# Layer 0 of a two-layer decoder trunk: low parts through ScalarE and adding transfers, wide products from group 4 on, matmuls in runs of three

## The chip, the cores and the metric

The kernel runs on one core of one Trainium2 chip. The metric is the device time of one execution in microseconds (us); less is better. The engines are TensorE (PE, with its weight loads listed apart as PEld), VectorE (DVE), ScalarE (ACT), GpSimd (POOL) and SyncE (SP). Here POOL and SP mostly issue transfers.

## The reference

A causal two-layer trunk runs over 512 positions of width 1024 in float32. Each layer is a residual mixer and then a gated feed-forward block; the change touches the feed-forward block of layer 0 alone.

```python
D_MODEL, SEQ, D_FF, DEPTH = 1024, 512, 2816, 2

def gated_conv_ffn(x, w_gate, w_up, conv_w, conv_b, w_down):
    g = jnp.einsum('bsd,df->bsf', x, w_gate)
    g = causal_dwconv3(g, conv_w) + conv_b
    up = jnp.einsum('bsd,df->bsf', x, w_up)
    return jnp.einsum('bsf,fd->bsd', jax.nn.silu(g) * up, w_down)

for layer in range(DEPTH):
    h = h + mixer(rms_norm(h, norm_mix[layer]))
    h = h + gated_conv_ffn(rms_norm(h, norm_ffn[layer]), ...)
return rms_norm(h, final_norm)
```

## The kernel before

**Precision.** Every float32 operand is split into a high part `hi` (rounded to the matmul's input type) and a low part `lo = x - hi`. A product is `hi*hi + hi*lo + lo*hi`. The split is made in two ways. `halves` and `split`: ACT copies `hi`, DVE subtracts `lo`. `summed`: ACT writes `lo = -x` rounded, a transfer on POOL's queue adds x to it in memory (`accum_op=ALU.add`), and ACT copies `hi`; DVE has no part in it.

**Feed-forward block (class `Ffn`).** The 2816 hidden rows are 22 tiles of 128. They are computed in steps f = 0, 2, 4, ..., 20 of two tiles each (`STEPS`). Step 0 is computed directly. In the others gate (`g`) and up (`u`) each take seven block products instead of eight (a Winograd form of Strassen's scheme on 2 x 2 blocks): `prepare(f)` builds weight sums (`s12`, `s34`), `block_sums(kp)` builds the sums of the token blocks (`t41`, `t23`) once, and `products(f)` multiplies. The seven products of a key share three PSUM banks a, b and e (`BANK`); the running sum in bank a or e must be copied out (evacuated) before the next product of that bank begins. ACT copies the first half of a bank to `rows` or `kept` (line 944), DVE adds what is to be added (line 932).

**Narrow and wide.** In a narrow product (line 705) each of four k-tiles takes three matmuls of 256 columns. In a wide one (line 695) the moving operand holds `hi` and `lo` side by side: one matmul of 512 columns with the weight's high part and one of 256 columns with its low part, so 8 instructions for 12. The second half of the bank must then be added too, one more DVE instruction of 128x256. `FIRST_WIDE[layer]` gives the step from which each key is wide (at the gate's first wide step, `u` is wide in products 2, 5 and 3 only).

**Order of the matmuls.** `todo` lists the 14 products of a step. In layer 0 the low matmuls of one product and the next stand together, then the high ones of two (runs of two); in layer 1, where all 14 are wide, runs of three low and three high parts alternate.

**After the products.** Convolution and SiLU give the activation rows `s`; `split_acts` calls `act`, which makes `a_hi` (ACT, line 265) and `a_lo` (DVE, line 267), four buffers of each. `half_down` projects rows already split through half of the output columns (`project`, lines 156 to 158; tile `d` in layer 0, `dn` in layer 1), after each step's products.

**What sets the order.** A scheduler fixes one order of instructions for each engine before the run; each engine takes its list strictly in that order. So an instruction that waits holds up all that stands behind it on its engine. Transfers of raw weights go through SP's queue as one of four `raw` buffers comes free; adding transfers go through POOL's.

Of the kernel before, what the change touches and what calls it, by code (L numbers as in the profile page):

```python
# [9 lines left out]
F32R = mybir.dt.float32r  # L10
BF16 = mybir.dt.bfloat16
AF = mybir.ActivationFunctionType
ALU = mybir.AluOpType
PSUM = bass.MemoryType.PSUM

P = 128
D = 1024
S = 512
# [3 lines left out]
NF = FF // P  # L22
# [9 lines left out]
def tile_trunk(ctx: ExitStack, tc: tile.TileContext, x, norm_mix, norm_ffn, final_norm,  # L32
# [3 lines left out]
    nc = tc.nc  # L36
# [44 lines left out]
    def behind(ins, first):  # L81

        if first is not None:
            tc.add_manual_dep(ins.ins, first.ins.name, mybir.DependencyInfo(
                mybir.DependencyClass.NoSync, mybir.DependencyReason.DATA), reason="order")
# [176 lines left out]
    def split(pool, src, name, scale=1.0, tag="a", bufs=None):  # L262
        hi = pool.tile([P, S], F32R, tag=f"{tag}hi", bufs=bufs, name=f"{name}_hi")
        lo = pool.tile([P, S], F32R, tag=f"{tag}lo", bufs=bufs, name=f"{name}_lo")
        nc.scalar.activation(hi, src, AF.Copy, scale=scale)  # L265
        if isinstance(scale, float):
            nc.vector.tensor_tensor(lo, src, hi.bitcast(F32), ALU.subtract)
        else:
            nc.vector.scalar_tensor_tensor(lo, src, scale, hi.bitcast(F32),
                                           op0=ALU.mult, op1=ALU.subtract)  # L270
        return hi, lo
# [15 lines left out]
    def padded_tile():  # L287
        turn[0] += 1
        return padded[turn[0] % NPADDED]
# [382 lines left out]
    PAIRS = [k for i in range(NP) for k in (i, i + NP)]  # L672

    FIRST_BY_DMA = 4
    FIRST_WIDE = ({"g": 6, "u": 8}, {"g": 4, "u": 6})

    BANK = {1: "a", 6: "a", 7: "a", 4: "a", 5: "e", 3: "e", 2: "b"}

# [37 lines left out]
    class Ffn:  # L716
# [33 lines left out]
            return s  # L750

        def act(self, ft, s):
            self.acts[ft] = split(self.ap, s, f"a{self.layer}_{ft}", tag="a", bufs=4)

        def pair_weights(self, order):

# [42 lines left out]
        def block_sums(self, kp):  # L799

            n, g1, h1 = f"{self.layer}_{kp}", self.prm("ffn", kp + NP), h[kp + NP]
            t = self.ap.tile([P, 4, HALF], F32, tag="sum", bufs=3, name=f"t{n}")
            b11, b12 = t[:, 2, :], t[:, 3, :]
            first = nc.scalar.activation(t[:, 2:, :], h[kp].rearrange("p (a b) -> p a b", a=2),
                                         AF.Copy, scale=self.prm("ffn", kp))
            if kp > 0:
                behind(first, self.first_sums)
            nc.vector.scalar_tensor_tensor(t[:, 1, :], h1[:, HALF:], g1, b12, op0=ALU.mult,
                                           op1=ALU.subtract)
            nc.vector.tensor_tensor(t[:, 0, :], t[:, 1, :], b11, ALU.add)  # L810
            nc.vector.tensor_tensor(b12, b12, b11, ALU.subtract)
            nc.vector.scalar_tensor_tensor(b11, h1[:, :HALF], g1, t[:, 0, :], op0=ALU.mult,
                                           op1=ALU.subtract)
            self.t23[kp] = self.sums(kp)
            t41 = self.ap.tile([P, 2, 2, HALF], F32R, name=f"t41_{n}")
            self.t41[kp], self.t41both[kp] = (t41[:, 0], t41[:, 1]), t41
            for (hi, lo), src in ((self.t41[kp], t[:, 2:, :]), *(
                    ((both[:, 0], both[:, 1]), t[:, i, :]) for i, both in enumerate(self.t23[kp]))):
                if kp > 1:
                    self.halves(hi, lo, src)  # L820
                    continue
                behind(nc.scalar.activation(lo, src, AF.Copy, scale=-1.0), self.first_sums)
                nc.gpsimd.dma_start(lo, src, accum_op=ALU.add)
                behind(nc.scalar.activation(hi, src, AF.Copy), self.first_sums)
# [87 lines left out]
        def products(self, f, stat):  # L912

            layer, ap, n = self.layer, self.ap, f"{self.layer}_{f}"
            banks = {"g": {}, "u": {}}
            kept = ap.tile([P, 3, HALF], F32, tag="kept", bufs=1, name=f"kept{n}")
            pads = [padded_tile() for _ in range(2)]
            lo, hi = slice(2, 2 + HALF), slice(2 + HALF, 2 + S)
            dst = {("g", 1): pads[0][:, lo], ("g", 6): pads[0][:, hi], ("g", 7): pads[1][:, hi],
                   ("g", 4): pads[1][:, lo]}  # L920
            dst.update({("u", product): kept[:, i, :] for i, product in enumerate((1, 6, 7))})
            onto = {2: 1, 7: 7, 3: 6}
            s = {}

            def in_both(key, product):
                first = FIRST_WIDE[layer]
                return f >= first[key] or f == first["g"] and product in (2, 5, 3)

            def add(d, bank, halves):
                ins = None  # L930
                for half in halves:
                    ins = nc.vector.tensor_tensor(d, bank[:, half * HALF : (half + 1) * HALF], d,
                                                  ALU.add)
                return ins

            def after(key, product, bank):
                halves = range(1 + in_both(key, product))
                if product in onto:
                    ins = add(dst[key, onto[product]], bank, halves)
                    if product == 7:  # L940
                        self.added[key] = ins
                elif (key, product) != ("u", 4):
                    d = dst[key, 7 if product == 5 else product]
                    nc.scalar.copy(d, bank[:, :HALF])
                    add(d, bank, halves[1:])

            todo = [("g", 1), ("u", 1), ("g", 2), ("g", 5), ("g", 6), ("u", 5), ("u", 6),
                    ("g", 7), ("u", 2), ("u", 7), ("g", 3), ("u", 3), ("g", 4), ("u", 4)]
            if layer and all(in_both(*at) for at in todo):
                parts_of = [(0, (False,))]  # L950
                for i in range(0, len(todo), 3):
                    parts_of += [(j, (True,)) for j in range(i, min(i + 3, len(todo)))]
                    parts_of += [(j, (False,)) for j in range(i + 1, min(i + 4, len(todo)))]
            else:
                parts_of = [(i, (i % 2 == 1, i % 2 == 0)) for i in range(len(todo))]
            begun = set()
            for i, lows in parts_of:
                key, product = todo[i]
                bank = self.multiply(banks[key], f"{key}{n}", product, stat[key, product],
                                     in_both(key, product), lows)  # L960
                if len(lows) == 1 and i not in begun:
                    begun.add(i)
                    continue
                after(key, product, bank)
                if (key, product) in (("g", 4), ("g", 3)):
                    j = product == 4
                    row = pads[j][:, 2:]
                    nc.vector.tensor_tensor(row, row, self.r, ALU.mult)  # L968
                    s[j] = self.silu(self.conv(pads[j], f + j), f + j)
                    if j and layer == 0:  # L970
                        nc.vector.tensor_tensor(s[1], s[1], self.r, ALU.mult)
            if layer == 0:
                nc.vector.tensor_tensor(kept[:, :2, :], kept[:, :2, :],
                                        self.r.rearrange("p (a b) -> p a b", a=2), ALU.mult)
            s0 = s[0].rearrange("p (a b) -> p a b", a=2)
            nc.vector.tensor_tensor(s0, kept[:, :2, :], s0, ALU.mult)
            nc.vector.tensor_tensor(s[1][:, HALF:], kept[:, 2, :], s[1][:, HALF:], ALU.mult)
            last = bank[:, :HALF]
            if in_both("u", 4):
                last = kept[:, 0, :]  # L980
                nc.scalar.copy(last, bank[:, :HALF])
                add(last, bank, (1,))
            nc.vector.tensor_tensor(s[1][:, :HALF], last, s[1][:, :HALF], ALU.mult)
            return [(f + 1, s[1]), (f, s[0])]
# [53 lines left out]
    def mixer1(norm):  # L1038
        w = w_in_odd[0]
        with tc.tile_pool(name="m1", bufs=1) as mp:  # L1040
# [156 lines left out]
            for kp in range(NP):  # L1197
                block_sums(kp)
# [144 lines left out]
    def ffn1(norm):  # L1343
        with tc.tile_pool(name="f1", bufs=1) as ap:
# [108 lines left out]
            def product(p, i, c0=0, c1=512, bank=None):  # L1453
# [14 lines left out]
                return ps  # L1468

            vec, act, pool = nc.vector, nc.scalar, nc.gpsimd  # L1470
            rows_f = [wp.tile([P, D], F32, tag="raw", bufs=4, name=f"yf{t}") for t in range(NT)]
            factor, root = ([ssf[:, t, i : i + 1] for t in range(NT)] for i in (4, 5))
# [181 lines left out]
```

## Time and profile before

| | |
|---|---|
| median of 3 runs | 966.77 us (966.71 to 966.88) |
| the profiled execution's own time | 966.66 us |
| its span, first to last instruction | 964.9 us |
| PE busy | 956.6 us (99%) |
| PEld busy | 826.5 us (86%) |
| DVE busy | 847.2 us (88%) |
| ACT busy | 620.8 us (64%) |
| POOL busy | 162.4 us (17%) |
| granted TensorE clock | 0.999 |

The products of layer 0 run from 165.99 us (step 2) to about 450 us (end of those of step 20), those of layer 1 from 644.78 us. Where one engine is busy for 99% of the span, a change moves the time only by what it takes from that engine's work or by the waits that it puts into it. A timeline row gives start, length, engine, line, operation, tiles and shape; lengths of matmuls that follow one another overlap, so distances between starts are what counts. Rows of POOL's own transfers show only the issue; the landing is in the list of transfers.

### The profile page before, as it was taken

What the parts mean: (1) busy time and instruction counts of PE and PEld (TensorE: products, weight loads), DVE (VectorE), ACT (ScalarE), POOL (GpSimd) and SP (SyncE); (2) the same over time, 40 slices, a digit from 0 to 9 for tenths busy, and PEclk for the clock granted to TensorE, in tenths of its full rate; (3) what the DMA queues carried; (4) which work ended last, traced back from release to release, by engine and by line L of the source; (5) the groups of instructions that cost most, each with busy time, mean ns of one, the idle gap of its engine ahead of it and who ended that gap; (6) DMA issues with size and microseconds to landing.
All of it is one profiled execution on the core that took longest, in us unless ns stands there. A gap on an engine that the chain in (4) does not pass through costs nothing.

```text
span 964.9 us, 14240 instructions
## 1 busy us (share of the span) xinstructions
PE 956.6 (99%) x5155; PEld 826.5 (86%) x5155; DVE 847.2 (88%) x1435; ACT 620.8 (64%) x944; POOL 162.4 (17%) x183
## 2 busy tenths in 40 slices
PE   9999999999999999999999999999999999999997
PEld 7888898998888888888888888989888888888885
DVE  6887988989899998998878689889998989989898
ACT  5524667766576565765487847787765566646676
POOL 2142333111011010110311002321111011110124
PEclk9999999999999999999999999999999999999999
DMA  7442345777777578774452323467776777667865
GB/s 253 146 141 87 66 144 120 179 188 178 176 174 176 153 175 197 164 180 137 131 153 88 109 88 88 138 134 184 186 181 175 182 176 174 167 168 177 207 146 152
DMA packets 95538, 150.47 MB, mean 156 GB/s; under 512 B 5252, under 2 KB 61548, under 8 KB 95468
## 3 DMA queue, kind: packets, MB, share of 16 engines
q1 hardware_dynamic: 77996, 98.69, 32.8%
q0 software_dynamic: 15696, 49.03, 27.8%
q10 hardware_dynamic: 1776, 1.84, 0.6%
q8 instruction: 41, 0.67, 0.3%
q14 instruction: 29, 0.24, 0.1%
HBM read 98.42 MB, written 2.10 MB: 104 GB/s over the span
## 4 chain that ended last, share of the span: by engine, by line
PE 99%; DMA 0%; DVE 0%; issue 0%; SPq 0%; ACT 0%; DVEq 0%
PE dn L156 3%; PE d L157 3%; PE d L156 3%; PE dn L157 3%; PE d L158 3%; PE dn L158 3%; PE vu_a L1166 2%; PE gu L156 2%; PE gu L158 2%; PE gu L157 2%; PE u_2a L705 1%; PE g_2a L705 1%; PE u_4a L705 1%; PE g_6a L695 1%; PE u_12a L695 1%; PE u_16a L695 1%
## 5 line engine op out<-in xcount | busy, mean ns | idle before, releaser
L143 POOL DMA_DIRECT2D wlo_g<-raw_g x20 | 17.2, 860 | 318.8 <-ACT wlo_g L141 66.5
L741 DVE SCALAR_TENSOR_TENSOR c<-rows,prm,c 128x512 f32<-128x512 f32 x88 | 64.9, 746 | 1.2 <-ACT c L739 1.0
L156 PE MATMUL d<-a_hi,whi_d 128*128 128x512 f32 x144 | 56.1, 389 | 0.0
L156 PE MATMUL dn<-whi_dn,a_hi 128*128 128x512 f32 x144 | 56.1, 389 | 0.0
L157 PE MATMUL d<-a_lo,whi_d 128*128 128x512 f32 x144 | 56.1, 389 | 0.0
L157 PE MATMUL dn<-wlo_dn,a_hi 128*128 128x512 f32 x144 | 56.0, 389 | 0.0
L158 PE MATMUL d<-a_hi,wlo_d 128*128 128x512 f32 x144 | 56.0, 389 | 0.0
L158 PE MATMUL dn<-whi_dn,a_lo 128*128 128x512 f32 x144 | 56.0, 389 | 0.0
L856 ACT ACTIVATE whi_a<-raw_g 128x512 fp32r<-128x512 f32 x20 | 12.6, 632 | 67.2 <-PE g_18e L695 9.4
L739 ACT ACTIVATE c<-rows,prm 128x512 f32<-128x512 f32 x44 | 31.3, 714 | 10.2 <-DVE rows L968 10.1
L1371 DVE SCALAR_TENSOR_TENSOR y<-dn,small,y 128x512 f32<-128x512 f32 x40 | 28.0, 749 | 6.7 <-PE dn L158 6.7
L749 ACT ACTIVATE s<-c,prm 128x512 f32<-128x512 f32 x44 | 31.4, 715 | 3.2 <-DVE c L741 3.0
L265 ACT ACTIVATE a_hi<-s 128x512 fp32r<-128x512 f32 x40 | 24.7, 626 | 12.2 <-PE d L158 9.4
L201 ACT ACTIVATE hg<-h,prm 128x512 fp32r<-128x512 f32 x24 | 17.2, 719 | 23.5 <-DVE h L314 17.0
L158 PEld LDWEIGHTS dn<-whi_dn,a_lo 128*128 128x128 f32 x144 | 27.0, 188 | 5.7
L158 PEld LDWEIGHTS d<-a_hi,wlo_d 128*128 128x128 f32 x144 | 27.0, 188 | 5.6
L157 PEld LDWEIGHTS dn<-wlo_dn,a_hi 128*128 128x128 f32 x144 | 27.0, 188 | 5.6
L156 PEld LDWEIGHTS d<-a_hi,whi_d 128*128 128x128 f32 x144 | 27.0, 188 | 5.6
L156 PEld LDWEIGHTS dn<-whi_dn,a_hi 128*128 128x128 f32 x144 | 27.0, 188 | 5.6
L157 PEld LDWEIGHTS d<-a_lo,whi_d 128*128 128x128 f32 x144 | 27.0, 188 | 5.5
L141 ACT ACTIVATE wlo_g<-raw_g 128x1024 fp32r<-128x1024 f32 x20 | 21.0, 1048 | 16.3 <-PE g_2e L705 7.6
L152 DVE TENSOR_TENSOR wlo_d<-raw_d,whi_d 128x1024 fp32r<-128x1024 f32 x18 | 22.0, 1224 | 10.4 <-ACT whi_d L151 10.4
(1279 smaller groups left out, 3377.6 us busy)
## 6 DMA issues: line engine op xcount, KB each, us to landing
raw_g<-in_w_ffn_gate_dram SPq DMA_DIRECT2D x40, 512.0 KB, 3.8
raw_u<-in_w_ffn_up_dram SPq DMA_DIRECT2D x40, 512.0 KB, 3.7
raw_dn<-in_w_ffn_down_dram SPq DMA_DIRECT2D x22, 512.0 KB, 3.5
wlo_g<-raw_g POOLq DMA_DIRECT2D x20, 512.0 KB, 5.2
wlo_u<-raw_u POOLq DMA_DIRECT2D x20, 512.0 KB, 6.1
raw_d<-in_w_ffn_down_dram SPq DMA_DIRECT2D x18, 512.0 KB, 4.1
wlo_s12g<-s12g POOLq DMA_DIRECT2D x18, 512.0 KB, 6.6
wlo_s34g<-s34g POOLq DMA_DIRECT2D x18, 512.0 KB, 6.2
```

Source lines behind the costliest of these rows:

```text
L141: first = nc.scalar.activation(lo, raw, AF.Copy, scale=-1.0)
L152: behind(nc.vector.tensor_tensor(lo, raw, hi.bitcast(F32), ALU.subtract), after[0])
L156: nc.tensor.matmul(ps, lhs[0], rhs[0], start=start, stop=False, skip_group_check=skip)
L157: nc.tensor.matmul(ps, lhs[0], rhs[1], start=False, stop=False, skip_group_check=skip)
L158: nc.tensor.matmul(ps, lhs[1], rhs[0], start=False, stop=stop, skip_group_check=skip)
L265: nc.scalar.activation(hi, src, AF.Copy, scale=scale)
L695: last_matmul[0] = nc.tensor.matmul(ps if low else banks[at], left(kp)[low], right(kp)[0] if low else both(kp), start=first, stop=kp == NP ...
L705: nc.tensor.matmul(ps, l, r, start=first, stop=end, skip_group_check=True)
L739: nc.scalar.activation(c, t[:, 0:S], AF.Copy, scale=prm("cf", ft))
L741: self.last_conv = nc.vector.scalar_tensor_tensor(c, t[:, i : S + i], prm("cf", i * NF + ft), c, op0=ALU.mult, op1=ALU.add)
L749: self.last_silu = nc.scalar.activation(s, c, AF.Silu, bias=self.prm("bf", ft))
L1371: return nc.vector.scalar_tensor_tensor(dst, ps, ffn.cols[:, t : t + 1], dst, op0=ALU.mult, op1=ALU.add)
```

## The change

Four edits, all in the feed-forward block of layer 0. (1) `FIRST_WIDE`: the gate is wide from step 4 (was 6), up from step 6 (was 8), as in layer 1. (2) Runs of three are used in layer 0 too, for every step that is wide throughout but step 20: steps 6 to 18. (3) `block_sums` takes the low parts of all four token sums by adding transfers (was: the first two). (4) `act` makes the low parts of rows 0 to 17 by ACT and an adding transfer (was: DVE).

```diff
-    FIRST_WIDE = ({"g": 6, "u": 8}, {"g": 4, "u": 6})
+    FIRST_WIDE = ({"g": 4, "u": 6}, {"g": 4, "u": 6})
...
         def act(self, ft, s):
-            self.acts[ft] = split(self.ap, s, f"a{self.layer}_{ft}", tag="a", bufs=4)
+            name = f"a{self.layer}_{ft}"
+            if not (self.layer == 0 and ft < NF - 4):
+                self.acts[ft] = split(self.ap, s, name, tag="a", bufs=4)
+                return
+            hi = self.ap.tile([P, S], F32R, tag="ahi", bufs=4, name=f"{name}_hi")
+            lo = self.ap.tile([P, S], F32R, tag="alo", bufs=4, name=f"{name}_lo")
+            first = nc.scalar.activation(lo, s, AF.Copy, scale=-1.0)
+            nc.gpsimd.dma_start(lo, s, accum_op=ALU.add)
+            behind(nc.scalar.activation(hi, s, AF.Copy), first)
+            self.acts[ft] = hi, lo
...
-                if kp > 1:
+                if kp > 1 and self.layer:
                     self.halves(hi, lo, src)
                     continue
                 behind(nc.scalar.activation(lo, src, AF.Copy, scale=-1.0), self.first_sums)
...
-            if layer and all(in_both(*at) for at in todo):
+            if (layer or f + 2 < NF) and all(in_both(*at) for at in todo):
                 parts_of = [(0, (False,))]
```

On PE, the first product of step 4 (`g_4a`, tokens `hg`, weights `whi_a`/`wlo_a`) stood so before:

```order
L705 MATMUL g_4a<-hg_111,whi_a_0_4_1946 128x256 x2
L705 MATMUL g_4a<-hg_111,wlo_a_0_4_1947 128x256
L705 MATMUL g_4a<-hg_112,whi_a_0_4_1946 128x256 x2
L705 MATMUL g_4a<-hg_112,wlo_a_0_4_1947 128x256
L705 MATMUL g_4a<-hg_113,whi_a_0_4_1946 128x256 x2
L705 MATMUL g_4a<-hg_113,wlo_a_0_4_1947 128x256
```

and with the change so:

```order
L695 MATMUL g_4a<-hg_111,whi_a_0_4_1954 128x512
L695 MATMUL g_4a<-hg_112,whi_a_0_4_1954 128x512
L695 MATMUL g_4a<-hg_113,whi_a_0_4_1954 128x512
L695 MATMUL g_4a<-hg_114,whi_a_0_4_1954 128x512
L695 MATMUL g_4a<-hg_111,wlo_a_0_4_1955 128x256
L695 MATMUL g_4a<-hg_112,wlo_a_0_4_1955 128x256
```

Pairs of 256 columns have become one matmul of 512, and the low ones follow in a block.

On POOL's queue, the transfers for step 10 (`wlo_...`: low parts of weights, `s12g` and `s34g` being the gate's weight sums) stood so before:

```order
L143 DMA wlo_g_10_1_2874<-raw_g_10_1_2857 128x1024
L888 DMA wlo_s12g_10_2872<-s12g_10_2867 128x1024
L888 DMA wlo_s34g_10_2884<-s34g_10_2868 128x1024
L143 DMA wlo_u_10_1_2894<-raw_u_10_1_2859 128x1024
L143 DMA wlo_g_12_1_3161<-raw_g_12_1_3144 128x1024
```

and with the change, where `a_6_lo` to `a_9_lo` are the low parts of activation rows:

```order
L143 DMA wlo_g_10_1_2849<-raw_g_10_1_2832 128x1024
L897 DMA wlo_s12g_10_2847<-s12g_10_2842 128x1024
L760 DMA a_7_lo<-s_7_2436 128x512
L897 DMA wlo_s34g_10_2859<-s34g_10_2843 128x1024
L760 DMA a_6_lo<-s_6_2413 128x512
L143 DMA wlo_u_10_1_2869<-raw_u_10_1_2834 128x1024
L760 DMA a_9_lo<-s_9_2723 128x512
L760 DMA a_8_lo<-s_8_2700 128x512
L143 DMA wlo_g_12_1_3136<-raw_g_12_1_3119 128x1024
```

Two of the four new transfers stand ahead of the last weight transfers of step 10, two behind them. Steps 14 and 18 read the same.

On ACT, the end of the preparation of step 6 and its first copies out of PSUM (`rows`, `kept`) stood so before (`s_5` is the SiLU of row 5):

```order
L749 ACTIVATE s_5_2179<-c_5_2175,prm_415 128x512
L141 ACTIVATE wlo_u_6_1_2293<-raw_u_6_1_2258 128x1024
L856 ACTIVATE whi_s12u_6_2290<-s12u_6_2287 128x1024
L145 ACTIVATE whi_u_6_1_2292<-raw_u_6_1_2258 128x1024
L265 ACTIVATE a_5_hi<-s_5_2179 128x512
L265 ACTIVATE a_4_hi<-s_4_2146 128x512
L944 COPY rows_119<-g_6a 128x256
L944 COPY kept_6_2305<-u_6a 128x256
L944 COPY rows_119<-g_6e 128x256
L856 ACTIVATE whi_s34u_6_2301<-s12u_6_2287 128x1024
```

and with the change:

```order
L141 ACTIVATE wlo_u_6_1_2275<-raw_u_6_1_2240 128x1024
L865 ACTIVATE whi_s12u_6_2272<-s12u_6_2269 128x1024
L145 ACTIVATE whi_u_6_1_2274<-raw_u_6_1_2240 128x1024
L749 ACTIVATE s_5_2157<-c_5_2153,prm_415 128x512
L953 COPY rows_119<-g_6a 128x256
L953 COPY kept_6_2287<-u_6a 128x256
L759 ACTIVATE a_5_lo<-s_5_2157 128x512
L761 ACTIVATE a_5_hi<-s_5_2157 128x512
L759 ACTIVATE a_4_lo<-s_4_2130 128x512
L761 ACTIVATE a_4_hi<-s_4_2130 128x512
L865 ACTIVATE whi_s34u_6_2283<-s12u_6_2269 128x1024
L953 COPY rows_119<-g_6e 128x256
```

The SiLU of row 5 has moved behind three weight conversions, and four row instructions stand between it and the conversion `whi_s34u` and the copy of `g_6e`.

## The prediction

> **What bounds the kernel now.** I read the page first: busy times, then the chain that ended last.
>
> ```profile
> span 964.9 us, 14240 instructions
> PE 956.6 (99%) x5155; PEld 826.5 (86%) x5155; DVE 847.2 (88%) x1435; ACT 620.8 (64%) x944; POOL 162.4 (17%) x183
> PE 99%; DMA 0%; DVE 0%; issue 0%; SPq 0%; ACT 0%; DVEq 0%
> ```
>
> The chain is PE work from end to end. A busy PE proves little by itself, since ends of matmuls are modelled; so I next took PE's own list of waits, which is these two rows, both at the start of the program:
>
> ```profile
> PE clock L58 <- PEq L1640: 0.8, 1, 0.8
> PE z L417 <- ACT whi_z L410: 0.3, 1, 0.3
> ```
>
> So the edits that relieve DVE buy nothing directly: PE does not wait for DVE in any sum worth the name. What can be gained is PE's own time in layer 0's products; what can be lost is a new wait of PE. About 0.2% of the time, 1.9 us, is what a measurement of this kernel surely tells from no change.
>
> **Part 1: wide products one group sooner.** Layer 1 already runs with the setting that layer 0 gets, so the price need not be guessed: the length of the same stage in layer 1 is the length to come. From the timeline of PE, the starts of the first product and of the first projection matmul, step 4 and then step 6, each for layer 0 and layer 1:
>
> ```profile
> 191.45 0.40 PE L705 MATMUL g_4a<-hg,whi_a 128*128 128x256 f32 x2
> 211.60 0.40 PE L156 MATMUL d<-a_hi,whi_d 128*128 128x512 f32 x1
> 670.24 1.07 PE L695 MATMUL g_4a<-hg,whi_a 128*128 128x512 f32 x4
> 689.93 0.40 PE L156 MATMUL dn<-whi_dn,a_hi 128*128 128x512 f32 x1
> ...
> 217.07 1.07 PE L695 MATMUL g_6a<-hg,whi_a 128*128 128x512 f32 x4
> 237.10 0.40 PE L156 MATMUL d<-a_hi,whi_d 128*128 128x512 f32 x1
> 695.40 1.07 PE L695 MATMUL g_6a<-hg,whi_a 128*128 128x512 f32 x4
> 714.92 0.39 PE L156 MATMUL dn<-whi_dn,a_hi 128*128 128x512 f32 x1
> ```
>
> Step 4: 20.15 us in layer 0, 19.69 in layer 1, so 0.46 saved (ten products become wide). Step 6: 20.03 against 19.52, so 0.51 saved (the last four products, runs of three, and a slip told below). The chain's rows agree on one product: narrow, wide with its low part first, wide with its high part first.
>
> ```profile
> 167.43 1.44 PE u_2a L705 x12
> 249.55 1.41 PE u_8a L695 x8
> 250.96 1.38 PE g_8b L695 x8
> ```
>
> On average 1.395 against 1.44, 0.045 each: 10 x 0.045 = 0.45 for step 4, as read above.
>
> Here a page of the Trainium skill speaks against the gain: "TensorE: Matmul & The Clock Gate", section "Back-to-back issue gap", gives an isolated gap of N/2.4 + 2.5 ns. By it a narrow product is 12 x 109.2 = 1310 ns and a wide one 4 x (109.2 + 215.8) = 1300 ns, 10 ns less; an estimate from the page is then 14 x 0.010 = 0.14 us for the whole change. The trace disagrees with this fivefold in its rows of 1.44 and 1.38 to 1.41, and I go by the trace.
>
> **Part 2: runs of three, steps 8 to 18.** The period from a step to the next, from the chain, layer 0 in runs of two and layer 1 in runs of three (the first row stands above):
>
> ```profile
> 432.20 1.41 PE u_20a L695 x8
> 744.07 1.41 PE u_8a L695 x8
> 926.43 1.41 PE u_20a L695 x8
> ```
>
> Layer 0: (432.20 - 249.55) / 6 = 30.442; layer 1: (926.43 - 744.07) / 6 = 30.393. Six steps save 6 x 0.049 = 0.29 us. Step 20 keeps its order. Parts 1 and 2 together: 0.46 + 0.51 + 0.29 = 1.26 us.
>
> **Part 3: what the changes load and relieve.** The durations, from DVE's and ACT's groups:
>
> ```profile
> L267 DVE TENSOR_TENSOR a_lo<-s,a_hi 128x512 fp32r<-128x512 f32 x2 | 1.4, 688 | 0.0
> L932 DVE TENSOR_TENSOR rows<-g_8a,rows 128x256 f32<-128x256 f32 x5 | 2.1, 420 | 0.0
> L265 ACT ACTIVATE a_hi<-s 128x512 fp32r<-128x512 f32 x40 | 24.7, 626 | 12.2 <-PE d L158 9.4
> ```
>
> DVE loses 18 rows x 0.69 and six token sums (two of 128x512, four of 128x256: 2 x 0.69 + 4 x 0.42), 15.5 us; it gains 14 adds x 0.42 = 5.9 us. Ten of these fall into step 4, where only two rows' subtractions leave (1.4): net 2.8 us more. ACT gains 18 x 0.63 + 2 x 0.63 + 4 x 0.4 = 14.2 us, hidden by its slack, which the windows of steps 4 and 6 show:
>
> ```profile
> 191.45:217.07 25.62, 25.62 (x193) 24.66 (x192) 22.36 (x37) 18.09 (x28) 3.44 (x4) 1.00 0.82 197
> 217.07:248.00 30.93, 30.89 (x177) 26.97 (x176) 28.30 (x52) 20.51 (x29) 4.30 (x5) 1.00 0.78 186
> ```
>
> (PE, PEld, DVE, ACT, POOL busy, clock, DMA share, GB/s.) In step 4 DVE goes from 22.4 to 25.2 of 25.2 us as written, though its order lets some of that run over into step 6, which has 2.6 us free. This is the tightest place. In step 6 the order on ACT puts `a_5_lo` ahead of `whi_s34u` and of the copies of `g_6e` and the next bank a; `a_5_lo` waits for the finished row 5, whose SiLU now stands three conversions later. If that is late, ACT's copy and DVE's add of product 6 are late, and PE's product 7 waits for the bank. Step 6 had such a slip already:
>
> ```profile
> 223.16 0.40 PE L695 MATMUL u_6e<-t,whi_s12u 128*128 128x512 f32 x1
> 223.60 1.19 PE L695 MATMUL g_6a<-t,whi_s12g 128*128 128x512 f32 x4
> DVE rows L932: 0.4, 1
> ```
>
> (The last row is what line 695 sat idle for.) The start is 0.44 after the one before it, where 0.23 is one matmul's pitch, so 0.2 lost; the row itself says up to 0.4. Similar places are step 2, where ACT's four row instructions stand ahead of two copies of `u`, and step 4. Bounds of the new waits: none at all, as in layer 1's steps 4 and 6 (their lengths above), to three slips of 0.4, 1.2 us. A gain below nothing is excluded, since layer 1's lengths hold no wait to remove. I take one slip, 0.2 us, because the row nearest in place, step 6 of layer 0 itself, shows one. Net gain: 1.26 - 0.2 = 1.06 us.
>
> **Part 4: the transfers.** 24 more on POOL's queue: 18 + 2 of 256 KB and 4 of 128 KB, 5.8 MB.
>
> ```profile
> q0 software_dynamic: 15696, 49.03, 27.8%
> t<-t POOLq DMA_DIRECT2D x4, 256.0 KB, 3.7
> wlo_u<-raw_u POOLq DMA_DIRECT2D x20, 512.0 KB, 6.1
> ```
>
> 0.278 x 964.9 / 49.03 = 5.5 us of the 16 engines per MB, so two rows in step 4 (0.52 MB) take 2.9 us there, and its share of 0.82 goes to about 0.93. A row lands between 3.7 us (256 KB) and 6.1 (512 KB); I take 4.5, nearer to its own size, as the queue is fuller. From row 2 on, rows are needed a whole set of products, some 19 us, after their split; rows 0 and 1 are split in the middle of step 2 and needed at its end. They cost nothing while that cover holds; where it is gone, each late transfer costs its lateness. In step 2 the six token sums stand ahead of the gate's weights:
>
> ```profile
> 156.49 0.86 POOL L143 DMA_DIRECT2D wlo_g<-raw_g  x1 [3.15 <-ACT wlo_g L141]
> 168.87 1.44 PE g_2b L705 x12
> ```
>
> Six issues of 0.86 move `wlo_g` to 161.7, its landing to 167.8, ahead of 168.87 by 1.1: covered, but not by much.
>
> What queues behind them matters more. On POOL the weight transfers `wlo_s34g` and `wlo_u` of steps 10, 14 and 18 now stand behind `a_7_lo` and `a_6_lo` (and their like), whose buffers come free as the running projection reads them. Before:
>
> ```profile
> 277.79 0.86 POOL L888 DMA_DIRECT2D wlo_s34g<-s34g  x1 [8.68 <-ACT wlo_s34g L887]
> 279.69 0.86 POOL L143 DMA_DIRECT2D wlo_u<-raw_u  x1 [1.04 <-ACT wlo_u L141]
> 270.99 0.61 ACT L265 ACTIVATE a_hi<-s 128x512 fp32r<-128x512 f32 x1
> 273.20 0.63 ACT L265 ACTIVATE a_hi<-s 128x512 fp32r<-128x512 f32 x1
> 276.45 1.04 ACT L887 ACTIVATE wlo_s34g<-s34g 128x1024 fp32r<-128x1024 f32 x1
> 278.44 1.07 PE L695 MATMUL g_10a<-hg,whi_a 128*128 128x512 f32 x4
> 725.81 1.07 PE L695 MATMUL g_8a<-hg,whi_a 128*128 128x512 f32 x4
> 736.03 0.64 PE L695 MATMUL u_8b<-hg,wlo_u 128*128 128x256 f32 x4
> ```
>
> In runs of three `wlo_u` is wanted 736.03 - 725.81 = 10.22 us into the products, at 288.66. Issued at 279.69 it lands at 285.8. The first two rows got their buffers by 273.2, while the weights' conversion came only at 276.45, behind a third row. Now it stands behind these two alone, so I expect `wlo_u` to be issued near 277 and to land near 284: no wait.
>
> **The sum.** The profiled execution took 966.66 us, 1.76 more than its span, and the median of the runs is 0.11 above it. 966.77 - 1.06 = 965.71, so 965.7.
>
> **Rivals.** *Late weights in steps 10, 14 and 18 (slower).* If the second row's buffer is free only at the projection's end, 278.44, then two row instructions (0.63 each), two conversions of 1.04, 6.1 to land and 3.7 behind the row's own transfer give 278.44 + 1.26 + 2.08 + 6.1 + 3.7 = 291.6, 2.9 late, three times 8.7 us: 966.77 - 1.26 + 8.7 = 974.2. It decides once `wlo_u` is issued after 288.66 - 6.1 = 282.5. For it: a DMA share that comes near 0.9. Against it: the starts of 270.99 and 273.20. The Trainium skill, "DMA: Bandwidth & Descriptors", section "Anatomy of one DMA", fits 2.0 us plus bytes / 436e3, an estimate of 2.6 us for a row and 3.2 for 512 KB, which would leave still more room. The trace disagrees, with 3.7 and 6.1 us.
>
> *Evacuations late in steps 2 to 6.* The three slips at their bound: 966.77 - 1.26 + 1.2 = 966.7; if half of DVE's 2.8 us in step 4 shows on PE too, 968.1. For it: DVE without slack in step 4. Against it: ACT has 7 us free there, and layer 1 does the same adds.
>
> *Columns alone count.* Both forms stream 3072 columns a product; if layer 1's shorter stages came from something else, as the page on TensorE would have it, nothing is gained: 966.6 to 966.8. The rows of 1.44 and 1.395 inside layer 0 speak against it.
>
> *A hidden wait goes with DVE's load.* At most the profile's leftovers, another microsecond: 964.7. PE's list of waits speaks against it.
>
> **How the numbers follow.** Forecast 0.68 (965.3 to 966.1); late evacuations 0.15; late weights 0.10; columns alone 0.04; hidden wait 0.03. A range of 965.2 to 967.6 leaves out the last and late weights and a part of the late evacuations, under 0.2. Slower by over 0.2% (above 968.7): late weights, with a remainder of the evacuations, 0.11; faster by over 0.2% (below 964.8): 0.03; the rest, 0.86, is within 0.2%.
>
> **What would show it.** In the new trace: step 4's products 19.7 us long, step 6's 19.5 (19.7 with a slip), periods of 30.39 from step 8 to 18; PE's waits for DVE `rows` under 0.5 us in all; `wlo_u` of step 10 issued ahead of the end of the projection; rows' transfers near 4.5 us. A DVE that is busy to the full in step 4 with PE starts of more than 0.23 apart would mean the second rival; gaps ahead of `u_10b` or the low part of `g_10a` would mean the first, and that I misread when buffers come free.

## The result, and the profile after

The changed kernel took 968.66 us (median of 21 runs, 966.2 to 972.54) and the kernel before 966.55 us (21 runs, 966.09 to 967.62): a ratio of 1.0024, with a 95% interval of 1.0018 to 1.003. It is slower, by 2.1 us at the medians, and outside the predicted range; its runs scatter over 6 us where those of before scatter over 1.5. Its profiled execution took 970.49 us, so the profile shows one of its longer runs.

From the page after: span, busy times, the chain, POOL's queue.

```profile
span 968.8 us, 14225 instructions
PE 957.3 (99%) x5099; PEld 824.4 (85%) x5099; DVE 840.6 (87%) x1425; ACT 630.3 (65%) x969; POOL 183.6 (19%) x207
PE 86%; DVE 5%; DMA 4%; issue 2%; ACT 2%; POOL 1%; DVEq 0%; SPq 0%; POOLq 0%; ACTq 0%
q0 software_dynamic: 19152, 54.80, 31.3%
```

PE's sum is 0.7 us more than before although the products got shorter, and 14% of the chain is no longer PE. PE's list of waits after has four rows more than before:

```profile
PE u_8b L695 <- DMA wlo_u<-raw_u: 1.6, 1, 1.6
PE clock L58 <- PEq L1649: 0.8, 1, 0.8
PE g_6a L695 <- DVE rows L941: 0.8, 1, 0.8
PE u_6e L695 <- DVE wlo_s12u L866: 0.5, 1, 0.5
PE u_2a L705 <- ACT kept L953: 0.4, 1, 0.4
```

From PE's timeline after, the first product and the first projection matmul of steps 6 and 8:

```profile
217.96 1.07 PE L695 MATMUL g_6a<-hg,whi_a 128*128 128x512 f32 x4
239.36 0.39 PE L156 MATMUL d<-a_hi,whi_d 128*128 128x512 f32 x1
250.24 1.07 PE L695 MATMUL g_8a<-hg,whi_a 128*128 128x512 f32 x4
271.58 0.39 PE L156 MATMUL d<-a_hi,whi_d 128*128 128x512 f32 x1
```

Read so for each step, the products last (us; the last column runs from the start of step 2's products to the start of step 20's; in the timeline of before step 2 starts at 165.83, and 165.99, given above, is its row in the chain):

| kernel | step 2 | 4 | 6 | 8 | 10 to 18 | 2 to 20 |
|---|---|---|---|---|---|---|
| before | 20.15 | 20.15 | 20.03 | 19.55 | 19.55 to 19.57 | 264.83 |
| after | 21.04 | 19.94 | 21.40 | 21.34 | 19.50 to 19.51 | 268.40 |
| forecast | 20.15 | 19.69 | 19.7 | 19.5 | 19.5 | 263.77 |

Steps 10 to 18 are as forecast. Against the forecast, the loss is in steps 2 (0.9), 4 (0.25), 6 (1.7) and 8 (1.8), in a run that is 1.8 us longer than the median.

**Step 8.** ACT's timeline, before and then after; the rows in brackets end with what the engine waited for:

```profile
233.66 1.04 ACT L141 ACTIVATE wlo_g<-raw_g 128x1024 fp32r<-128x1024 f32 x1
236.61 0.73 ACT L739 ACTIVATE c<-rows,prm 128x512 f32<-128x512 f32 x1 [0.38 <-DVE rows L968]
```

```profile
239.18 0.72 ACT L739 ACTIVATE c<-rows,prm 128x512 f32<-128x512 f32 x1 [0.65 <-DVE rows L977]
241.76 0.72 ACT L739 ACTIVATE c<-rows,prm 128x512 f32<-128x512 f32 x1 [1.86 <-DVE rows L977]
242.39 1.04 ACT L141 ACTIVATE wlo_g<-raw_g 128x1024 fp32r<-128x1024 f32 x1
```

Before, the first weight conversion of step 8 stood ahead of step 6's convolutions; now it stands behind both, and both wait for DVE. So POOL's four weight transfers of step 8 go out within 7 us instead of 11. The first and last issue before, then after, and `wlo_u`'s landing in the list of transfers of this stretch, before and after:

```profile
234.99 0.86 POOL L143 DMA_DIRECT2D wlo_g<-raw_g  x1 [15.95 <-DVE rows L932]
246.24 0.86 POOL L143 DMA_DIRECT2D wlo_u<-raw_u  x1 [1.04 <-ACT wlo_u L141]
...
wlo_u<-raw_u POOLq DMA_DIRECT2D x1, 512.0 KB, 6.9
```

```profile
243.73 0.86 POOL L143 DMA_DIRECT2D wlo_g<-raw_g  x1 [16.06 <-DVE c L741]
250.91 0.86 POOL L143 DMA_DIRECT2D wlo_u<-raw_u  x1 [1.03 <-ACT wlo_u L141]
...
wlo_u<-raw_u POOLq DMA_DIRECT2D x1, 512.0 KB, 11.2
...
262.20 0.74 PE L695 MATMUL u_8b<-hg,wlo_u 128*128 128x256 f32 x4 [1.58 <-DMA wlo_u<-raw_u]
```

It lands at 250.91 + 11.2 = 262.1; it is wanted 10.22 after 250.24, at 260.5: PE's 1.6 us.

**Step 6.** Its loss begins 30 us sooner, in the weights of step 4, and comes by two paths. The first is a buffer that comes free late. An adding transfer reads its raw buffer until it lands, and there are four raw buffers. SP's waits from 190 to 210 us, one row before and one after:

```profile
SPq L129 <- DMA wlo_u<-raw_u: 1.3, 1, 1.3
```

```profile
SPq L129 <- DMA wlo_u<-raw_u: 4.1, 1, 4.1
```

Step 4's `wlo_u` took 5.4 us before and 7.9 after. It landed at 194.24 + 7.9 = 202.1, and only then, at 202.31, SP's second `raw_g` for step 6 went out (before: 198.53). The second path is a load that is itself slow. From the timelines after, in order of time:

```profile
196.93 0.86 POOL L760 DMA_DIRECT2D a_lo<-s  x1 [1.83 <-ACT kept L953]
197.68 0.37 SPq L129 DMA_DIRECT2D raw_u<-in_w_ffn_up_dram  x1
198.24 0.86 POOL L760 DMA_DIRECT2D a_lo<-s  x1 [0.45 <-ACT a_lo L759]
206.34 0.63 ACT L865 ACTIVATE whi_a<-raw_u 128x512 fp32r<-128x512 f32 x1 [2.93 <-DMA raw_u<-in_w_ffn_up_dram]
207.00 0.69 DVE L866 TENSOR_TENSOR wlo_a<-raw_u,whi_a 128x512 fp32r<-128x512 f32 x1 [3.13 <-ACT whi_a L865]
224.57 0.37 ACT L953 COPY kept<-u_6a 128x256 f32<-128x256 f32 x1 [2.28 <-DVE s L986]
226.41 0.74 PE L695 MATMUL g_6a<-t,wlo_s12g 128*128 128x256 f32 x4 [0.77 <-DVE rows L941]
```

The `raw_u` that ACT waits for went out at 197.68, before `wlo_u` had landed, so it did not wait for that buffer; it lies beside the two rows' transfers. ACT could use it at 206.34, 8.7 us after its issue; before, ACT used it 5.75 us after its issue (196.69 to 202.44) without a wait. ACT waits 2.93 us for it, DVE 3.13 us for ACT, with step 4's sums and rows queued behind it; then ACT's copy of `u_6a` waits for step 4's last row, and PE for the bank.

### The profile page after: what moved, and what is told of

Same layout as the page of the kernel before. It is cut to its first block, busy times and chain, and to the rows that moved or that the text cites. A ratio compares the mean times of both kernels' runs of the same rounds, so it can differ in the third digit from the quotient of the medians.

```text
span 968.8 us, 14225 instructions
## 1 busy us (share of the span) xinstructions
PE 957.3 (99%) x5099; PEld 824.4 (85%) x5099; DVE 840.6 (87%) x1425; ACT 630.3 (65%) x969; POOL 183.6 (19%) x207
## 4 chain that ended last, share of the span: by engine, by line
PE 86%; DVE 5%; DMA 4%; issue 2%; ACT 2%; POOL 1%; DVEq 0%; SPq 0%; POOLq 0%; ACTq 0%
PE dn L156 3%; PE dn L158 3%; PE dn L157 3%; PE d L156 3%; PE d L158 3%; PE d L157 3%; PE vu_a L1175 2%; DMA wlo_u<-raw_u 1%; PE u_20a L695 1%; PE u_18a L695 1%; PE u_16a L695 1%; PE g_16a L695 1%; PE u_12a L695 1%; PE g_12a L695 1%; PE g_18a L695 1%
## 5 line engine op out<-in xcount | busy, mean ns | idle before, releaser
L212 POOL TENSOR_TENSOR ssq_m<-ssq_m,sq_m 128x512 f32<-128x512 f32 x14 | 19.7, 1406 | 65.2 <-ACT sq_m L211 65.2
L202 DVE SCALAR_TENSOR_TENSOR hg<-h,prm,hg 128x512 fp32r<-128x512 f32 x24 | 24.7, 1031 | 5.2 <-ACT hg L201 5.1
```

The costliest lines, as they stand in the source:

```text
L202: nc.vector.scalar_tensor_tensor(hg[k][1], h[k], g, hg[k][0].bitcast(F32), op0=ALU.mult, op1=ALU.subtract)
L212: nc.gpsimd.tensor_tensor(self.ssq, self.ssq, sq, ALU.add)
```

## The experiments

Each quoted text is what was expected before the run. Times are medians of 5 to 11 runs, with the ratio to the kernel before on the same chip and its 95% interval; the granted clock of the profiled runs was 0.996 to 0.999.

**Parts alone (e1 to e4).** e1: edits 1 and 2 only. e2: edit 4 only. e3: the change without edit 3. e4: edits 1 and 2, and rows 6 to 17 by transfer:

```diff
-            if not (self.layer == 0 and ft < NF - 4):
+            if not (self.layer == 0 and 5 < ft < NF - 4):
```

> Edits 1 and 2 alone: wide from step 4 and runs of three; rows and token sums as before. Theory A (the rows' low parts by ScalarE and adding transfers make the loss, the matmul edits bring what layer 1's stages promised): 966.55 - 1.26 = 965.3 us, steps 4 and 6 at 19.7 and 19.5 us, no wait of PE over 0.3 us. Theory B (the ten more adds of step 4 overload VectorE and the evacuations come late whatever makes the low parts): 967 to 969 us, with PE waiting for VectorE's rows in step 6.

> Edit 4 alone: low parts of rows 0 to 17 by ScalarE and adding transfers, all else as before. Theory A: slower than before by 2 to 4 us (968.5 to 970.5), with PE waits in steps 2, 6 and 8 as in the whole change. Theory B: no wait, 966.2 to 966.6 us, since VectorE is relieved and nothing is added to it. Theory C (the token sums are the cause): 966.5 us.

> The whole change without edit 3 (token sums 2 and 3 as before, by VectorE). Theory A: still 968 to 969 us, as the whole change. Theory C (six more transfers ahead of the gate's weights and twelve more ScalarE instructions shift step 2 and all behind it): 965.3 to 966 us.

> Edits 1 and 2, and edit 4 for rows 6 to 17 only; rows 0 to 5 and the token sums as before. Theory A in its narrow form (it is the rows split in steps 2 to 6, where ScalarE's list puts them ahead of PSUM copies): 965.3 to 965.6 us and no PE wait over 0.3. In its wide form (256 KB adding transfers crowd the queue wherever they stand): 967 to 968.5 us, with PE waiting for weights in a step from 8 on.

Measured: e1 971.17 us, 1.0052 (1.0039 to 1.0064); e2 968.53, 1.0023 (1.0013 to 1.0033); e3 968.37, 1.0022 (1.001 to 1.0033); e4 968.55, 1.0024 (1.0014 to 1.0033). Three of PE's waits in e1:

```profile
PE u_8b L695 <- DMA wlo_u<-raw_u: 1.5, 1, 1.5
...
PE u_10e L695 <- DVE wlo_s12u L857: 0.5, 1, 0.5
...
PE g_14a L695 <- DVE rows L932: 0.3, 1, 0.3
```

The kernel without any new transfer is the slowest, so the new transfers are not needed to make step 8 late. Its steps 4 and 6 are 19.72 and 19.52 long, as forecast; steps 10, 14, 16 and 18 take 20.2 to 20.8, which the row transfers of e3 and e4 bring back to 19.51. PE's one new wait in e2 is 2.4 us at `g_6a`; in e4 there are two, 2.0 at `u_8b` and 1.1 at `u_6b`, both for `wlo_u`. e3 is about as slow as the change, so edit 3 is not the main cause.

**The two edits on PE apart (e5, e6).**

> Only the table of the first wide products is changed; runs of two, row splits and token sums as before. Theory L (late list): with step 6 all wide, the order on ACT puts step 8's conversion of wlo_g behind a row copy and the first convolution of step 6, so step 8's four weight transfers bunch; that is seen here too: wlo_g issued after 236 (before: 234.99), wlo_u landing 9 us or more after its issue. Runs of two want wlo_u 12.1 us into the products and not 10.2, so the wait for it is 0 to 0.5. Step 4 19.7, step 6 19.5 to 19.7, steps 10 to 18 as before (period 30.44): 965.6 to 966.3 us. Rival T (runs of three alone make the late weights): wlo_u lands within 7 us here.

> Only the order of products in layer 0 is changed to runs of three (steps 8 to 18). The order on ACT keeps step 8's wlo_g ahead of the copies of step 6, as before. Theory L: wlo_u of step 8 issued near 246.2, landing by 254, wanted at 258.2, no wait for it at u_8b. Rival T: runs of three want it 1.9 us sooner and that suffices: u_8b waits 1 to 2 us. For steps 10 to 18, theory D (runs of three cost DVE's or ACT's copies their slack in layer 0, where each row has one multiplication more than in layer 1): 0.6 to 0.9 us lost a step, five steps, as in the run of edits 1 and 2 alone: 969.5 to 971 us. Rival of D (those slips were left over from step 8's delay): 966.2 us.

Measured: e5 968.44, 1.0016 (1.0007 to 1.0025); e6 967.61, 1.0009 (1.0 to 1.0018). In e6 `wlo_u` of step 8 went out at 245.56, landed in 5.6 us, and `u_8b` waits for nothing, so runs of three do not make the late weights. e5 bunches the transfers without them (237.16, then 244.74 to 249.48; `wlo_u` 8.7 us). There PE did not wait for `wlo_u`, which landed at 258.2 and in runs of two is wanted 12.1 us into the products, at 259.5; so the loss at `u_8b` takes both edits, the late list and the earlier use. But its raw buffer came free late: SP's `raw_u` went out at 258.35 (before: 253.24) and `raw_g` right behind it at 258.82, and DVE stood still.

```profile
264.49 0.69 DVE L877 TENSOR_TENSOR s12g<-raw_g,raw_g 128x512 f32<-128x512 f32 x1 [2.50 <-DMA raw_g<-in_w_ffn_gate_dram]
```

Step 10 then lost 1.66 us (waits for DVE `rows`), and step 14 lost 1.53 in the same way, where DVE waited 2.63 us for `raw_g` after step 12's `wlo_u` had taken 8.5. The forecast of 965.6 to 966.3 missed this path. e6 loses 0.45 each in steps 14 and 18 (19.96 and 19.97), where PE waits 0.2 for DVE `rows`: theory D had 0.6 to 0.9 in five steps, so it holds for two steps and at a smaller size.

**The list put right (e7, e12).** e7 is the whole change, e12 edits 1 and 2, each with ACT's conversion of step 8's `wlo_g` tied ahead; nothing else is touched (the three lines of the edit that set the order; the comments name the instructions):

```diff
+                if key == "g" and f == 8 and layer == 0:
+                    behind(self.copied, last_first[0])       # last copy of g_6a
+                    behind(self.c_first[6], last_first[0])   # convolution of row 6
```

> The whole change, and ACT's conversion of step 8's wlo_g is tied ahead of the last copy and the first convolution of step 6, as it stood before the change; nothing else is touched. Theory L: wlo_g of step 8 issued some 6 us sooner than in the changed kernel, the four transfers spread over 10 us or more, wlo_u lands 7 us after its issue or less, and PE's 1.6 us at u_8b go; step 8's products fall from 21.3 to 19.6. 968.66 - 1.7 = 967.0 us. Rival (contention by the rows' transfers makes wlo_u late): the wait at u_8b stays over 1 us, 968.7 us.

> Wide products one group sooner and runs of three, as in the run of these two alone (e1, 971.17 us), with step 8's wlo_g tied ahead; all rows and sums by DVE. If step 8's delay is all that is wrong, its 1.5 us wait goes and the slips of steps 10 to 18 with it: 965.5 us. If the slips are DVE's own (runs of three alone lost 0.45 in steps 14 and 18), 0.4 to 1 us a step are lost in several steps: 967 to 969.5 us.

Measured: e7 967.57 us, 1.0003 (0.9994 to 1.0012); e12 967.21, 1.0002 (0.9993 to 1.0012). Step 8 is 19.51 in both, and in e7 `wlo_g` goes out at 237.40 and `wlo_u` lands in 6.3 us. So the order of ACT's list is the cause of step 8's loss, shown by moving one instruction. In e12 steps 10 to 18 are 19.51 too, but for 14 and 18 (20.24 and 20.35), where PE waits 0.3 for DVE `rows` each: e1's other slips came from step 8, these two are DVE's own.

**What the row transfers are good for (e8, e9).** e8: runs of three, and rows 8 to 17 by transfer, the rest as before. e9: edits 1 and 2, the list as in e7, and rows 8 to 17 by transfer.

> Runs of three in layer 0 (steps 8 to 18), low parts of rows 8 to 17 by ScalarE and adding transfers; rows 0 to 7, token sums and the table of wide products as before. Theories L and D together: no wait at u_8b since the list keeps wlo_g ahead, no slips in steps 10 to 18 since DVE is relieved there, steps of 30.40: 966.5 - 0.3 = 966.2 us, PE's list of waits empty but for the start. If the rows' transfers are what harms, waits for wlo_u come back in steps 10, 14 or 18 and the time is 967.5 or more.

> Wide products one group sooner and runs of three, low parts of rows 8 to 17 alone by ScalarE and adding transfers, token sums as before, and step 8's conversion of wlo_g tied ahead of the last copy and the first convolution of step 6. Theory L and D (the loss of each part is a list out of step or a copy late): every wait is gone, step 4 is 19.7, step 6 19.5, steps 8 to 18 19.5: the whole 1.26 of the forecast against the kernel before, 965.3 us (964.9 to 965.8). Rival (the table of wide products brings slips of its own downstream whatever DVE's load): PE waits for DVE rows in steps 10 and 14, 966.5 us or more.

Measured: e8 966.28 us, 0.9992 (0.9983 to 1.0001); e9 965.91 us, 0.999 (0.9981 to 0.9999). PE's whole list of waits in e9:

```profile
PE clock L58 <- PEq L1657: 0.8, 1, 0.8
```

Its steps are 20.15, 19.71, 19.52 and 19.51 long, and from step 2 to step 20 it takes 263.56 us, 1.27 less than before; the prediction's Parts 1 and 2 say 1.26. This version is faster than both kernels; against the one before by 0.9 us at the medians, with an interval that ends just short of 1.

**Which of the early rows and sums (e10, e11).** e10: e7 without edit 3. e11: e9 with edit 3.

> The whole change with step 8's wlo_g tied as in the run before (e7), and without the edit on the token sums. If the sums' four ScalarE instructions put step 2 late by 0.6 to 0.9, step 2's products are 20.15 long here and the wait for the copy kept at u_2a is gone; step 6 keeps its wait for DVE rows (0.4 to 0.8) from the rows 2 to 5. Time 966.6 us, against 967.6 with the sums. Rival (the four row instructions alone make step 2 late): step 2 stays at 20.8.

> As e9, with the token sums by ScalarE and adding transfers as in the change; rows 0 to 7 by DVE as before. If rows 0 and 1 are what put ACT's copies late in step 2, step 2 is 20.15 here although the sums are as in the change, and if rows 2 to 5 are what puts step 6 late, step 6 is 19.5: 965.3 us, as e9. Rival (the sums alone): step 2 20.5 or more, 965.8 to 966.2 us.

Measured: e10 967.05 us, 0.9999 (0.999 to 1.0007); e11 967.36, 1.0003 (0.9994 to 1.0012). Step 2 is 20.16 and 20.25, against 20.79 in e7, so only the two together lose there: the sums put ACT's list late at `whi_s34u` of step 2 (by 0.9 us in the changed kernel, 0.7 in e7, both against e10), and the four instructions of rows 0 and 1 carry that into the copy that `u_2a` waits for. e10 keeps the loss of step 6 (21.09, ACT's wait for `raw_u` 2.6). e11 was expected at 965.3 and missed: step 4 took 20.28, and step 6 took 20.62 with a wait of 0.8 for step 6's own `wlo_u`. The sums need not be the reason. e4, which has neither them nor a row's transfer ahead of step 8, has the same wait (1.1): step 6's `wlo_u` went out 0.35 ahead of the products in e1, e4, e9 and e11 alike, and took 6.9 us in e1 and e9 but 8.5 and 8.3 in e4 and e11. What makes the difference stays open.

**Transfers or ScalarE (e13 to e16).** Into e9, for rows 2 to 5: e13 adds a plain transfer, e14 a ScalarE copy, both to a tile that nothing reads (three lines of `act`; the comment gives e14's).

```diff
+                if self.layer == 0 and 1 < ft < 6:
+                    dead = self.ap.tile([P, S], F32, tag="dead", bufs=1, name=f"{name}_dead")
+                    nc.gpsimd.dma_start(dead, s)             # e14: nc.scalar.activation(dead, s, AF.Copy)
```

e15 is e9 with rows 2 and 3 in the changed way too, e16 e9 with all rows of the change but these two.

> The kernel of e9 (no waits of PE behind its start), and for rows 2 to 5 a plain 256 KB transfer of the row into a tile that nothing reads, issued on POOL's queue at the place of the change's a_lo; low parts and token sums stay with DVE. Theory C (contention): raw_u of step 6 lands 2 us or more later than in e9, ACT's conversion whi_a<-raw_u of step 6 and DVE behind it wait 2 to 3 us near 203 us, step 6's products are 20.5 to 21.4 long instead of 19.52, and the time is 966.9 to 967.6 us. Rival A (ACT's instructions): step 6 stays at 19.5 and the time at 965.9 us.

> The kernel of e9, and for rows 2 to 5 one more copy of the row by ScalarE into a tile that nothing reads; no transfer is added. Theory C (contention): step 6 stays within 0.3 us of 19.52, 965.9 to 966.2 us. Rival A (ACT's instructions ahead of the copies): step 6 is 20.5 or longer, 966.9 us or more.

> The kernel of e9 with rows 2 and 3 too by ScalarE and adding transfers; rows 0, 1 and 4 to 7 and the token sums stay with DVE. Theory C (rows 2 and 3 lie beside step 6's raw loads): ACT's whi_a<-raw_u waits 1.9 to 2.9 us for the load near 202 to 205 us, the DMA share from 195.5 to 204.7 is near 1.05 instead of 0.84, step 6 loses 0.5 us or more against 19.52, and the time is 966.5 to 967.3 us. Rival (rows 4 and 5, ahead of the copies of step 6): no wait for raw_u, step 6 at 19.5, 965.9 us.

> The kernel of e9 with rows 0, 1 and 4 to 7 too by ScalarE and adding transfers; rows 2 and 3 and the token sums stay with DVE. Theory C: no wait for raw_u at step 6, step 6 within 0.3 us of 19.5, 965.7 to 966.2 us. Rival: step 6 20.5 or longer through the four row instructions ahead of its copies, 966.7 us or more.

Measured: e13 966.84 us, 0.9996 (0.9987 to 1.0005); e14 965.65, 0.9986 (0.9977 to 0.9994); e15 966.94, 0.9999 (0.999 to 1.0008); e16 965.73, 0.9989 (0.998 to 0.9998). The single runs fall into two groups. In e13 seven of eleven lie at 966.8 to 967.1 and four at 965.4 to 966.0; in e15 seven at 966.9 to 967.6 and four at 965.4 to 965.9; in e16 ten at 965.3 to 966.1 and one at 967.04; in e14 all eleven at 964.9 to 966.0; in e9 eight at 965.4 to 966.0 and three at 966.5 to 966.8. So with transfers of rows 2 and 3 most runs are longer by some 1.2 us, and ACT's instructions cost nothing.

The profiled runs of e13 and e15 were of the lower group (step 6 19.52 and 19.91; ACT's wait for `raw_u` none and 0.2), so the expected waits are not seen there. Two other profiles show each path of step 6 alone. That of e16 was its one long run: without rows 2 and 3 ACT waits for no `raw_u`, but step 4's `wlo_u` took 7.8 us, SP's second `raw_g` went out at 201.05, DVE waited for it, and step 6 took 20.66.

```profile
206.84 0.69 DVE L889 TENSOR_TENSOR s12g<-raw_g,raw_g 128x512 f32<-128x512 f32 x1 [1.94 <-DMA raw_g<-in_w_ffn_gate_dram]
```

In e2 `wlo_u` took 5.6 us, but ACT waited 1.93 us for `raw_u`, and step 6 took 22.37.

Over the 18 profiles, step 4's `wlo_u` landed in 7.2 to 7.9 us in five (after, e3, e10, e11, e16), and step 6 took 20.6 to 21.4 in all of them; in the thirteen others it landed in 5.4 to 6.4, and step 6 took 20.03 or less in all but e2, e4 and e7. ACT's wait for `raw_u` is in all six profiles with rows 2 and 3 by adding transfer (0.2 to 2.9), e2 and e7 among them, and in no other.

The late `wlo_u` has a forerunner. In the same five profiles, and only there, step 4's `wlo_g` took 6.9 to 7.2 us (5.9 to 6.3 in the others), and SP's first `raw_g` for step 6, which waits for that buffer, went out 0.95 to 1.22 us ahead of step 4's products and not 1.80 to 2.24. The six profiles with rows 0 and 1 by transfer all have 6.3 or more, and of the rest only e11, with the sums, does. So the lateness seems to be handed on from step 2 from buffer to buffer; what decides between 6.3 and 7 us was not tried.

The shares of the DMA engines (last but one) from 195.5 to 204.7 us, in e9 and in e10:

```profile
195.50:204.70 9.20, 9.20 (x61) 8.33 (x60) 9.06 (x18) 4.86 (x9) 0.00 (x0) 1.00 0.84 215
```

```profile
195.50:204.70 9.20, 9.20 (x59) 8.22 (x58) 6.15 (x11) 5.32 (x11) 1.72 (x2) 1.00 1.05 246
```

The engines have no time left in e10, and DVE is busy 6.15 us where it was 9.06: it has less to do and stands still. A full share is not enough by itself, though: it was 1.06 in e15's profile too. So both paths are shown in the profiles, and the price of rows 2 and 3 by the runs; that the two groups of runs are the late and the early landings is likely, but no kernel was profiled in both.

## Why the prediction was wrong

**Parts 1 and 2** held: step 4 19.71 and step 6 19.52 in e9 against 19.69 and 19.52, 19.50 to 19.51 in steps 8 to 18, 1.27 in all against 1.26. Columns alone do not count here. The formula for an isolated gap in the Trainium skill, "TensorE: Matmul & The Clock Gate", section "Back-to-back issue gap", would have given an estimate of 0.14 for the whole change; the page itself says that this formula misses the spacing in a stream of weight loads and matmuls, and e9's steps 4 and 6 alone gained 0.95.

**Part 3** is a step that failed, in size and in mechanism. One slip of 0.2, at most 1.2, was put on steps 2 to 6, for DVE's load in step 4 and for a late SiLU of row 5 ahead of step 6's copies. Step 2 lost 0.89, step 4 0.25, step 6 1.88 against 19.52: 3.0 us in the profiled run. DVE's load was not the reason. e1 leaves DVE the rows that the change takes off it; DVE is busy 24.5 of 25.2 us in step 4, and steps 4 and 6 run as forecast. The prediction had the changed kernel at 25.2 of 25.2; there DVE was busy 21.4 of 25.4 us and stood still 3.13 us for ACT. Row 5 was late in step 6, as the text feared, but because ACT and then DVE had waited for a load. ACT's 7 us of free time, which the text took as cover, cover nothing that stands behind a waiting instruction in its list. The text did name the copies of `u` in step 2 behind the rows' instructions, where PE's 0.4 at `u_2a` lies; it did not see that the sums make them late.

**Part 4** failed in three ways. First, the row transfers were put at 4.5 us, and they take 7.4. From the list of transfers after:

```profile
a_lo<-s POOLq DMA_DIRECT2D x18, 256.0 KB, 7.4
t<-t POOLq DMA_DIRECT2D x6, 256.0 KB, 4.2
```

Token sums of the same size took 4.2, so the size alone does not make the time. The estimate of 2.6 us from the Trainium skill, "DMA: Bandwidth & Descriptors", section "Anatomy of one DMA", is further off. Secondly, "they cost nothing while that cover holds" looked only at who needs the rows, and along POOL's queue. The share of 0.82 going to 0.93 was worked out and given no price: measured, 0.85 went to 1.06 from 195.5 to 204.7 us, and the price was paid on SP's queue: by a raw load that took 8.7 us beside the rows' transfers, and by the next, whose buffer an adding transfer still read. Thirdly, ACT's order ahead of step 8 was not looked at, only that of step 6 and POOL's of step 10.

**The rival of late weights** had the right kind of wait, `wlo_u` at the low part of `u`, in the wrong place. It was put on steps 10, 14 and 18, where `wlo_u` of step 10 went out at 282.77, 0.3 behind the start of the products instead of 1.4 ahead of it as expected, took 6.6, and landed at 289.4, in time for 282.47 + 10.22 = 292.7. It came in step 8, from an instruction moved on ACT by edit 1, and e1 shows it without any row's transfer. The chance of 0.11 for over 0.2% slower priced three places and the bounds of three separate slips; that a late transfer delays the next step's loads, and so passes from step to step, was in no rival.

## What to carry to other kernels

Where a scheduler writes a fixed list for each engine, compare the order of every engine for two steps behind the edit, and look for conversions that feed a transfer and have slipped behind an instruction that waits. An adding transfer holds the buffer that it reads until it lands: count its lateness on the loads that want that buffer next, not only on the instruction that reads its result. Before moving work from an engine to transfers, look which raw loads lie in the same stretch and which engine waits for them next: rows 2 and 3, beside the loads of step 6, cost here, and rows 8 to 17 paid (1.3 us, e9 against e12).

## What the runs showed of the hardware

Within the changed kernel's profile the landing time of a 512 KB adding transfer of weights (`wlo_u`) went from 4.5 to 11.2 us; step 8's took 11.2 where the four transfers stood close together, and 6.3 in e7, where they were spread. Over the 18 profiles that of step 4's `wlo_u` came in two groups, 5.4 to 6.4 and 7.2 to 7.9 us, with nothing between. Full DMA engines alone cost nothing in e9: with a share of 1.08 from 338 to 348 us, and row transfers of 7.8 us at the median of all ten, PE waits for nothing.

```profile
338.00:348.00 10.00, 10.00 (x60) 8.82 (x59) 7.62 (x13) 6.79 (x12) 1.81 (x3) 1.00 1.08 223
...
a_lo<-s POOLq DMA_DIRECT2D x10, 256.0 KB, 7.8
```
